# Seven products of blocks for the keys and values of two heads, in a decoder step with split-precision matmuls

## The chip, the core and the metric

The kernel runs on one core of one Trainium2 chip. The metric is the device time of one launch in microseconds, as the median of several runs. A core has a matmul engine (TensorE, PE in the profile), VectorE (DVE), ScalarE (ACT), GpSimd (POOL) and a queue that issues DMAs (SP). Each engine takes its instructions in the order in which they are written in its own queue, and waits at an instruction until what it needs has been signalled.

## The reference

One inference step of a decoder layer. A prompt of 512 tokens, with 16 meta tokens ahead of it, and 8 sequences of 4 new tokens go through one layer. All 560 tokens share one input projection:

```
h = RMSNorm_pre(x)
[q,k,v,ga | cb,cc,ch,gc | ma,mc] = h @ w_in          # 2048 x 12288
a = StickBreakingAttn(q,k,v) * silu(ga)              # 8 heads of 128
c = cb * conv3_causal(cc * ch) * silu(gc)
m = sigmoid(ma + b_ga) * (a @ w_pa) + sigmoid(mc + b_gc) * (c @ w_pc)
x = x + RMSNorm_post(m @ w_out)
```

The new tokens attend to cached keys and values in pages of 128, too. Keys and values of all tokens are outputs of their own, so k and v are computed for all 560 tokens; the other parts of the projection are needed for 544 (not for the meta tokens).

## The kernel before

**Precision.** Every float32 operand x of a matmul is split into a high part (ACT casts it, L240 for weights) and a low part (DVE subtracts, L241), and a product is three matmuls: high x high, high x low, low x high. h stands in two tiles, `h_hi` and `h_lo`, of 16 chunks of 128 rows by 560 tokens.

**Plain products.** `proj` (through `gemm_into`, L256) makes one tile of 128 columns of `w_in`: two blocks of weights of 1024 x 128 are loaded by SP into `raw`, split into `whi` and `wlo`, and 16 chunks x 3 matmuls are run for each half of the tokens, 280 columns wide. That is 96 matmuls. `k_proj` and `v_proj` evacuate the result into a tile `raw` of the pool `heads`, transpose it on PE (`natural`), write it out, and keep it in DRAM (`k_scr`, `vn_scr`) for attention later. Heads 0 to 3 attend at once (`head_now`); heads 4 to 7 are only projected here (`head_later`).

**Products of blocks.** From the gates on, two column tiles are made together by `pair` and `seven` (matmuls at L941): w_in's rows and columns and h's rows and tokens are cut in halves, and the 2 x 2 block product is done with seven block products in place of eight, each of 8 chunks x 3 = 24 matmuls. For this the weights are added up by DVE into `s` and in place (L953, L956, L964, L969), seven blocks are split in place of four, and three sums of blocks of h stand ready: `t_hi[i]`, `t_lo[i]`, i = 0 to 2. A fourth sum, `r1`, takes the place of one block of h itself (its rows 0 to 1023, second half of the tokens). In `seven`, two products go to PSUM tiles named mm and the others to the one tile named o, the accumulator y: first with t[0], then with t[1], then with t[2]. Results leave by ACT, or by a subtraction on DVE (L967, L972).

**The block sums** (L908 to L925) are made in four chunks c of two of the eight chunks of rows: nine additions or subtractions and three splits for t[0] to t[2], and at the end one split of r1 into h. That is 13 DVE instructions a chunk. The last split overwrites a block of h that `proj` reads, so it has to wait until the last plain product has read it.

**Decode.** The new tokens' logits against cached keys are made on DVE in 64 steps (L754), which `dec_step` puts between the pieces of the rest: the first part beside the heads (`"part"`), the second beside the gates. Later, beside the products with `w_pc`, PE multiplies the weights with the cached value pages (`vpage`, L841), 64 pages of 128 x 512, loaded by POOL from a pool with 7 buffers; the four sequences of a group write to four different parts of PSUM tile tp.

**Order.** The kernel is written as one program; a list scheduler of the framework orders each engine's queue by priorities and by its own estimate of times, so that work of a later piece can stand ahead of an earlier one. What the queues look like is known from the built program.

Of the kernel before, what the change touches and what calls it, by code (L numbers as in the profile page):

```python
# [9 lines left out]
F32 = mybir.dt.float32  # L10
# [38 lines left out]
SCRATCH = 4096  # L49
FIRST = 4  # L50
WARM = 10
NOW = 4
LNEXP = "natural_log_exp_and_others"
SCALE = P ** -0.5
# [6 lines left out]
def hybrid_step_kernel(  # L61
# [209 lines left out]
    def proj(c, ranges):  # L271
        return gemm(weights(win_srcs(c)), h_rhs, ranges)
# [285 lines left out]
        split_evac(vhi[0:16, 4, :], vlo[0:16, 4, :], vn[0:16, 4, :], vn[0:16, 4, :])  # L558
        return vhi, vlo

    def k_proj(h):
        o = proj(GATE_K + h * P, ALL)
        kr = hp.tile([P, T], F32, name="raw", bufs=2)
        for ob, s in nparts(o):
            act.copy(kr[:, s], ob)
        kn = hp.tile([P, 5, P], F32, name="nat", bufs=2)
        ks = hp.tile([TS, P], F32, name="ks", bufs=1)
        natural(kr, kn, ks)
        outputs(k_prompt, k_sample, h, kn, ks, pin if h == 0 else lambda x: x)
# [7 lines left out]
    def v_proj(h, pl=None):  # L577
        o = proj(GATE_V + h * P, ALL)
        vr = hp.tile([P, T], F32, name="raw", bufs=2)
        for ob, s in nparts(o):  # L580
            act.copy(vr[:, s], ob)
# [150 lines left out]
    def decode_steps():  # L732
# [89 lines left out]
        for g in range(2):  # L822
            for hf in range(2):
                cs = slice(hf * 512, (hf + 1) * 512)
                po = t_ps()
                for pg in range(NPG + 1):
                    if pg < NPG:
                        vts = []
                        for j in range(4):
                            vt = d3.tile([P, 512], F32, name="vpage", bufs=7)  # L830
                            page_load(vt, vc, 4 * g + j, pg, cs)
                            vts.append(vt)
                        if g + hf + pg == 0:
                            yield "values"
                    for j in range(4):
                        bb = 4 * g + j
                        if pg < NPG:
                            lhs, rhs = A_all[:, pg, bb].rearrange("p h t -> p (h t)"), vts[j]
                        else:
                            lhs, rhs = An[:, bb, :], vflat[:, cs]  # L840
                        pe.matmul(po[32 * j:32 * (j + 1), :], lhsT=lhs, rhs=rhs, start=(pg == 0),  # L841
                                  stop=(pg == NPG), tile_position=(0, 32 * j), skip_group_check=True)
# [13 lines left out]
                yield  # L856
# [25 lines left out]
    for h in range(NOW):  # L882
        head_now(h)
    nctx.close()
    for h in range(NOW, H):
        head_later(h)
    dec_step(64, "part")

# [3 lines left out]
    t_hi, t_lo = [], []  # L892
    for i in range(3):
        ttp = tctx.enter_context(tc.tile_pool(name=f"tt{i}", bufs=1))
        t_hi.append(ttp.tile([P, 8, HU], F32R, name=f"t_hi{i}"))
        t_lo.append(ttp.tile([P, 8, HU], F32R, name=f"t_lo{i}"))
    h_f, l_f = h_hi.bitcast(F32), h_lo.bitcast(F32)

    def blk(x, i, j):
        return x[:, 8 * i:8 * i + 8, (j + 1) * HC - HU:(j + 1) * HC]  # L900

    def t_split(hi, lo, x):
        act.copy(hi, x)
        dve.tensor_sub(lo, x, hi.bitcast(F32))

    with tc.tile_pool(name="tsum", bufs=2, side="right") as tsp:
        r1 = tsp.tile([P, 8, HU], F32, name="r1", bufs=1)
        for c in range(0, 8, 2):  # L908
            def part(x, *ij):
                return (blk(x, *ij) if ij else x)[:, c:c + 2]  # L910

            r, x, y = part(r1), *(tsp.tile([P, 2, HU], F32, name=n) for n in "xy")
            dve.tensor_sub(r, part(h_f, 0, 0), part(h_f, 0, 1))
            dve.tensor_add(r, r, part(l_f, 0, 0))
            dve.tensor_sub(r, r, part(l_f, 0, 1))
# [11 lines left out]
    hctx.close()  # L927


    def gate_out(j, w, g):  # L930
        pool.dma_start(gate_scr[j][:, w, :], g)

    def gate_bias(j, w):
        return bg[:, KD * w + j:KD * w + j + 1]

    def product(o, w, rhs, start, stop):
        hi, lo = w
# [44 lines left out]
    def pair(c, n):  # L982
# [4 lines left out]
            return lambda k: (h_hi[:, 8 * i + k, slice(*hs[j])], h_lo[:, 8 * i + k, slice(*hs[j])])  # L987

        def rt(i):
            return lambda k: (t_hi[i][:, k, HU - n:HU], t_lo[i][:, k, HU - n:HU])  # L990

        ws = blocks_of(win, c)
        s = sp2.tile([P, 8, P], F32, name="s")
        yield from seven(ws, n, rb, rt, s, lambda name: sp2.tile([P, HU], F32, name=name)[:, :n])

    gctx = ExitStack()
    gp = gctx.enter_context(tc.tile_pool(name="gates", bufs=2))
    sp2 = gctx.enter_context(tc.tile_pool(name="sums", bufs=1))


    UP, US = PQ + 2, DB * (DT + 2)
# [95 lines left out]
    dec_step(64, "values")  # L1097
    assert "values" in dec_at and "end" not in dec_at
    gctx.close()
    tctx.close()  # L1100


# [329 lines left out]
```

## Time and profile before

| | us |
|---|---|
| median of 3 runs | 1615.59 (1614.0 to 1616.18) |
| profiled execution | 1616.69 |
| its span, first to last instruction | 1615.1 |
| PE busy | 1595.0 |
| DVE busy | 1268.6 |
| ACT busy | 754.0 |
| first matmul of blocks (L941) | at 369.3 |

The profile is of one execution. A page gives busy times and groups of instructions with their line in the kernel before; the chain of waits is followed back from the last instruction. "out<-in" are the program's tiles. The profile's own time is 1.6 us longer than its span.

### The profile page before, as it was taken

The numbers are of one execution on the slowest core, as the hardware profiler recorded it, in microseconds if no ns is written. First come the engines' busy times: TensorE is split into PE (matmuls) and PEld (weight loads), VectorE is DVE, ScalarE is ACT, GpSimd is POOL, SyncE is SP. The second block draws the span as 40 slices with busy tenths as digits, with TensorE's granted clock in tenths as the row PEclk, the third lists the DMA queues.
The fourth block names the chain that finished last, engine by engine and source line by source line (L and its number), as shares of the span: only waits on it lengthen the run. The fifth ranks groups of instructions, "written<-read, shape, count | busy, mean of one in ns | idle before, by whom it ended". The sixth has DMA issues, their size and how long they took to land.

```text
span 1615.1 us, 32344 instructions
## 1 busy us (share of the span) xinstructions
PE 1595.0 (99%) x12172; PEld 1533.7 (95%) x12172; DVE 1268.6 (79%) x3574; ACT 754.0 (47%) x1339; POOL 238.0 (15%) x428
## 2 busy tenths in 40 slices
PE   9999999999999999999999999999999999999997
PEld 8999999999999999999999999999757789999997
DVE  6328999947899999999999986667565747887776
ACT  6335554435444444444454444446554523355562
POOL 1133333221111001001011100001322210000000
PEclk9999999999999999999999999999999999999999
DMA  8245555344554445454455544444966755533345
GB/s 244 85 139 179 162 173 177 114 121 142 163 166 138 137 139 164 119 151 133 139 171 183 155 145 128 130 127 124 334 218 222 232 152 162 173 88 110 99 133 187
DMA packets 300675, 252.77 MB, mean 157 GB/s; under 512 B 11522, under 2 KB 268614, under 8 KB 299702
## 3 DMA queue, kind: packets, MB, share of 16 engines
q1 hardware_dynamic: 272021, 160.45, 34.5%
q0 software_dynamic: 28368, 89.98, 16.8%
q8 instruction: 95, 1.56, 0.4%
q14 instruction: 63, 0.51, 0.1%
q10 hardware_dynamic: 128, 0.27, 0.1%
HBM read 217.95 MB, written 32.71 MB: 155 GB/s over the span
## 4 chain that ended last, share of the span: by engine, by line
PE 95%; DMA 2%; DVE 2%; ACT 1%; issue 0%; DVEq 0%; POOL 0%; SPq 0%; ACTq 0%
PE mm L941 31%; PE mm L256 27%; PE o L941 23%; PE tp L841 3%; PE mm L321 2%; PE z L677 1%; PE o L687 1%; PE z L321 1%; PE z L608 1%; PE z L1373 1%; DMA sg<-a_scr 1%; PE tp L505 0%; DMA raw<-in_w_pc 0%; DMA qb<-q_scr 0%; PE z L1227 0%
## 5 line engine op out<-in xcount | busy, mean ns | idle before, releaser
L240 ACT CAST whi<-raw 128x1024 fp32r<-128x1024 f32 x247 | 259.5, 1051 | 385.2 <-PE mm L941 118.5
L241 DVE TENSOR_TENSOR wlo<-raw,whi 128x1024 fp32r<-128x1024 f32 x247 | 301.8, 1223 | 87.8 <-ACT whi L240 86.5
L941 PE MATMUL mm<-h_hi,whi 128*128 128x272 f32 (+1 forms) x1152 | 332.3, 288 | 0.0
L941 PE MATMUL mm<-h_lo,whi 128*128 128x272 f32 (+1 forms) x1152 | 332.3, 288 | 0.0
L941 PE MATMUL mm<-h_hi,wlo 128*128 128x272 f32 (+1 forms) x1152 | 332.3, 290 | 0.0
L941 PE MATMUL o<-t_hi,whi 128*128 128x272 f32 (+1 forms) x864 | 250.1, 289 | 1.6 <-DVE c L967 1.6
L941 PE MATMUL o<-t_lo,whi 128*128 128x272 f32 (+1 forms) x864 | 250.2, 290 | 0.0
L754 DVE CUSTOM_DVE_ANT_0 junk<-kpage,qb 128x128 f32<-128x128 f32 x1024 | 246.3, 288 | 4.7 <-DMA qb<-q_scr 4.3
L941 PE MATMUL o<-t_hi,wlo 128*128 128x272 f32 (+1 forms) x864 | 249.8, 289 | 0.0
L941 PEld LDWEIGHTS mm<-h_hi,whi 128*128 128x128 f32 x1152 | 217.4, 189 | 0.0
L941 PEld LDWEIGHTS mm<-h_hi,wlo 128*128 128x128 f32 x1152 | 216.8, 189 | 0.1
L941 PEld LDWEIGHTS mm<-h_lo,whi 128*128 128x128 f32 x1152 | 216.8, 188 | 0.1
L241 DVE TENSOR_TENSOR wlo<-s,whi 128x1024 fp32r<-128x1024 f32 x126 | 154.4, 1225 | 63.6 <-ACT whi L240 62.4
L240 ACT CAST whi<-s 128x1024 fp32r<-128x1024 f32 x126 | 132.0, 1048 | 153.8 <-PE mm L941 51.7
L256 PE MATMUL mm<-h_lo,whi 128*128 128x280 f32 (+1 forms) x640 | 187.6, 293 | 0.0
L256 PE MATMUL mm<-h_hi,wlo 128*128 128x280 f32 (+1 forms) x640 | 187.1, 293 | 0.0
L256 PE MATMUL mm<-h_hi,whi 128*128 128x280 f32 (+1 forms) x640 | 186.7, 292 | 0.0
L941 PEld LDWEIGHTS o<-t_hi,whi 128*128 128x128 f32 x864 | 163.0, 189 | 2.1 <-DVE c L967 2.0
L941 PEld LDWEIGHTS o<-t_lo,whi 128*128 128x128 f32 x864 | 163.4, 189 | 0.4 <-issue 0.4
L941 PEld LDWEIGHTS o<-t_hi,wlo 128*128 128x128 f32 x864 | 163.1, 189 | 0.1
L256 PEld LDWEIGHTS mm<-h_lo,whi 128*128 128x128 f32 x640 | 120.3, 188 | 0.8
L256 PEld LDWEIGHTS mm<-h_hi,whi 128*128 128x128 f32 x640 | 120.5, 188 | 0.5
(390 smaller groups left out, 3214.5 us busy)
## 6 DMA issues: line engine op xcount, KB each, us to landing
raw<-in_w_in SPq DMA_DIRECT2D x192, 512.0 KB, 4.3
kpage<-in_cache_k POOLq DMA_DIRECT2D x64, 256.0 KB, 3.7
qb<-q_scr POOLq DMA_DIRECT2D x32, 512.0 KB, 5.7
vpage<-in_cache_v POOLq DMA_DIRECT2D x64, 256.0 KB, 5.4
raw<-in_w_out SPq DMA_DIRECT2D x32, 512.0 KB, 4.1
gate_scr<-g POOLq DMA_DIRECT2D x32, 272.0 KB, 4.8
gt<-gate_scr POOLq DMA_DIRECT2D x16, 544.0 KB, 4.5
raw<-in_w_pc SPq DMA_DIRECT2D x16, 512.0 KB, 7.3
```

The costliest lines, as they stand in the source:

```text
L240: act.copy(hi, x)
L241: dve.tensor_sub(lo, x, hi.bitcast(F32))
L256: pe.matmul(o, lhsT=w, rhs=r[:, t0:t1], start=(k == 0 and n == 0), stop=(k == nk - 1 and n == 2))
L321: pin(pe.matmul(o, lhsT=l, rhs=r[:, k, t0:t1], start=(start and m == 0), stop=(stop and m == 2), skip_group_check=True))
L608: pe.matmul(zt[:m, c0:c0 + n], lhsT=l[:, s0:s0 + m], rhs=r[:, ts:ts + n], start=(c0 == 0 and i == 0), stop=(i == 2), skip_group_check=True)
L677: pe.matmul(o, lhsT=l, rhs=x, start=False, stop=(i == len(ops) - 1), skip_group_check=True)
L687: pe.matmul(ot[:, ts - NMETA:ts - NMETA + n], lhsT=l[:m, st, :], rhs=x[:m, c0:c0 + n], start=False, stop=(g == GROUPS[-1] and i == 2), ski ...
L754: dve.tensor_tensor_reduce(out=junk, in0=kt[:, h * P:(h + 1) * P], in1=qt[:, t, h * P:(h + 1) * P], scale=1.0, scalar=0.0, op0=ALU.mult, o ...
L841: pe.matmul(po[32 * j:32 * (j + 1), :], lhsT=lhs, rhs=rhs, start=(pg == 0), stop=(pg == NPG), tile_position=(0, 32 * j), skip_group_check= ...
L941: pe.matmul(o, lhsT=l[:, k, :], rhs=r, start=(start and k == 0 and m == 0), stop=(stop and k == 7 and m == 2), skip_group_check=True)
L1373: pin(pe.matmul(o, lhsT=(m1, m2)[h][:, k + 8 * (q == 1), ts], rhs=two[h][q == 2][:, :, k, :], start=(n == 0), stop=(n == 47)))
```

## The change

- Heads 6 and 7 (`PAIRED = 6`) no longer go through `head_later`. A new function `two_heads` makes the keys of both with one call of `pair` over all 280 tokens of each half, and then the values of both; `k_proj` and `v_proj` take the finished tile.
- The block sums cover all 280 columns of a half, not 274, so that `pair` can be called with 280. They stand behind heads 4 and 5 in the program, ahead of heads 6 and 7; before, they stood behind all heads.
- The pool of `seven`'s small tiles (`sums`) is opened ahead of the paired heads, and its tiles and the t tiles are 280 wide. The pool `vpage` has 6 buffers in place of 7.

```diff
+PAIRED = 6
+    def whole(c):
+        r = hp.tile([P, T], F32, name="raw", bufs=2)
+        for ob, s in nparts(proj(c, ALL)):
+            act.copy(r[:, s], ob)
+        return r
-    def k_proj(h):
-        o = proj(GATE_K + h * P, ALL)
-        kr = hp.tile([P, T], F32, name="raw", bufs=2)
-        for ob, s in nparts(o):
-            act.copy(kr[:, s], ob)
+    def k_proj(h, kr=None):
+        kr = whole(GATE_K + h * P) if kr is None else kr
...
-                            vt = d3.tile([P, 512], F32, name="vpage", bufs=7)
+                            vt = d3.tile([P, 512], F32, name="vpage", bufs=6)
...
-    for h in range(NOW, H):
+    for h in range(NOW, PAIRED):
         head_later(h)
     dec_step(64, "part")
...
-        t_hi.append(ttp.tile([P, 8, HU], F32R, name=f"t_hi{i}"))
-        t_lo.append(ttp.tile([P, 8, HU], F32R, name=f"t_lo{i}"))
+        t_hi.append(ttp.tile([P, 8, HC], F32R, name=f"t_hi{i}"))
+        t_lo.append(ttp.tile([P, 8, HC], F32R, name=f"t_lo{i}"))
...
-        return x[:, 8 * i:8 * i + 8, (j + 1) * HC - HU:(j + 1) * HC]
+        return x[:, 8 * i:8 * i + 8, j * HC:(j + 1) * HC]
...
+    def two_heads(c):
+        rs = [hp.tile([P, T], F32, name="raw", bufs=2) for _ in range(2)]
+        for m, half, ob in pair(c, HC):
+            act.copy(rs[m][:, NMETA + half * HQ:NMETA + (half + 1) * HQ], ob[:, HM:HC])
+            act.copy(rs[m][:, half * HM:(half + 1) * HM], ob[:, 0:HM])
+        return rs
+    for h in range(PAIRED, H, 2):
+        for i, r in enumerate(two_heads(GATE_K + h * P)):
+            pool.dma_start(k_scr[h + i], k_proj(h + i, r))
+        for i, r in enumerate(two_heads(GATE_V + h * P)):
+            v_proj(h + i, vr=r)
+    hctx.close()
```

How the queues move, at three places. Line numbers in the rows of the change are its own, one to two above those of before up to the sums, and 5 below them in `seven`.

DVE, the end of the block sums, before. r_5282 is r1; t_lo_5268, _5273 and _5278 are the low halves of t[0], t[1] and t[2]; x and y are the sums under way; the splits of `wlo<-raw` are those of plain products of heads.

```order
L904 TENSOR_TENSOR t_lo_5278<-x,t_hi_5277 128x548 x2
L510 COPY nat<-tp 16x128
L511 COPY ks<-tp 32x128
L241 TENSOR_TENSOR wlo<-raw,whi 128x1024 x2
L510 COPY nat<-tp 16x128
L511 COPY ks<-tp 32x128
L241 TENSOR_TENSOR wlo<-raw,whi 128x1024 x2
L510 COPY nat<-tp 16x128
L511 COPY ks<-tp 32x128
L904 TENSOR_TENSOR h_lo<-r_5282,h_hi 128x2x274 x4
L953 TENSOR_TENSOR s<-raw 128x1024
L964 TENSOR_TENSOR raw<-raw 128x1024
```

DVE, where r1 is split into h, in the change (the middle of the sums). r_4744 is r1; t_lo_4730, _4735 and _4740 are the low halves of t[0], t[1] and t[2]; `s` and the splits `wlo<-s` belong to the paired heads.

```order
L906 TENSOR_TENSOR h_lo<-r_4744,h_hi 128x2x280
L924 TENSOR_TENSOR x<-h_hi,x 128x560
L242 TENSOR_TENSOR wlo<-s,whi 128x1024
L906 TENSOR_TENSOR h_lo<-r_4744,h_hi 128x2x280
L924 TENSOR_TENSOR x<-h_hi,x 128x560
L906 TENSOR_TENSOR t_lo_4735<-y,t_hi_4734 128x560 x2
L925 TENSOR_TENSOR x<-x,h_lo 128x560
L951 TENSOR_TENSOR s<-s,raw 128x1024
L925 TENSOR_TENSOR x<-x,h_lo 128x560
L511 COPY nat<-tp 16x128
L512 COPY ks<-tp 32x128
L906 TENSOR_TENSOR t_lo_4740<-x,t_hi_4739 128x560
```

Before, the splits of weights of two whole heads stand between the last split of t[2] and the four splits of r1 into h, and the additions of weights for the first pair come behind. Now the splits of r1, the additions and splits of weights for the paired heads and the rest of the sums are mixed.

PE, the third product of the paired heads' keys in the change (tile o, with t[0]); before, PE runs plain products of heads 5 and 6 at this place of its queue.

```order
L936 MATMUL mm<-h_hi,wlo 128x280
L936 MATMUL o<-t_hi_4729,whi 128x280
L936 MATMUL o<-t_lo_4730,whi 128x280
L936 MATMUL mm<-h_hi,whi 128x280
L936 MATMUL mm<-h_lo,whi 128x280
L936 MATMUL o<-t_hi_4729,wlo 128x280
```

The product with t[0] now stands in pieces between pieces of other products.

PE, the last pages and the new tokens of one group in the stage of `w_pc`, before:

```order
L256 MATMUL mm<-c_hl,wlo 128x272
L677 MATMUL z<-lo,neg_u 128x400
L841 MATMUL tp<-vpage,z_all 32x512 x4
L841 MATMUL tp<-v_new,z_new 32x512 x4
L256 MATMUL mm<-c_hl,whi 128x272 x2
```

and a place of that stage in the change:

```order
L257 MATMUL mm<-c_hl,whi 128x272 x2
L843 MATMUL tp<-vpage,z_all 32x512
L257 MATMUL mm<-c_hl,wlo 128x272
L257 MATMUL mm<-c_hl,whi 128x272 x2
L257 MATMUL mm<-c_hl,wlo 128x272
L257 MATMUL mm<-c_hl,whi 128x272
L843 MATMUL tp<-vpage,z_all 32x512
```

Groups of value pages that stood together now stand apart in several places, and some that stood apart stand together.

More of the change, by code (lines that the diff above doesn't have):

```diff
@@ L575, in k_proj, with v_proj @@
         return kr
[L577 to L581, printed above, removed]
+    def v_proj(h, pl=None, vr=None):
+        vr = whole(GATE_V + h * P) if vr is None else vr
         vn = hp.tile([P, 5, P], F32, name="nat", bufs=2)
@@ L906, in hybrid_step_kernel @@
     with tc.tile_pool(name="tsum", bufs=2, side="right") as tsp:
-        r1 = tsp.tile([P, 8, HU], F32, name="r1", bufs=1)
+        r1 = tsp.tile([P, 8, HC], F32, name="r1", bufs=1)
         for c in range(0, 8, 2):
@@ L910, in part @@
                 return (blk(x, *ij) if ij else x)[:, c:c + 2]
-            r, x, y = part(r1), *(tsp.tile([P, 2, HU], F32, name=n) for n in "xy")
+            r, x, y = part(r1), *(tsp.tile([P, 2, HC], F32, name=n) for n in "xy")
             dve.tensor_sub(r, part(h_f, 0, 0), part(h_f, 0, 1))
@@ L926, in hybrid_step_kernel @@
             t_split(blk(h_hi, 0, 1)[:, c:c + 2], blk(h_lo, 0, 1)[:, c:c + 2], r1[:, c:c + 2])
[L927 to L934, printed above, removed]
     def product(o, w, rhs, start, stop):
@@ L989, in rt, with gate_out, gate_bias @@
         def rt(i):
-            return lambda k: (t_hi[i][:, k, HU - n:HU], t_lo[i][:, k, HU - n:HU])
+            return lambda k: (t_hi[i][:, k, HC - n:HC], t_lo[i][:, k, HC - n:HC])
         ws = blocks_of(win, c)
         s = sp2.tile([P, 8, P], F32, name="s")
-        yield from seven(ws, n, rb, rt, s, lambda name: sp2.tile([P, HU], F32, name=name)[:, :n])
+        yield from seven(ws, n, rb, rt, s, lambda name: sp2.tile([P, HC], F32, name=name)[:, :n])
+    sctx = ExitStack()
+    sp2 = sctx.enter_context(tc.tile_pool(name="sums", bufs=1))
+    def two_heads(c):
[10 more added lines that the diff above has]
+    hctx.close()
+    def gate_out(j, w, g):
+        pool.dma_start(gate_scr[j][:, w, :], g)
+    def gate_bias(j, w):
+        return bg[:, KD * w + j:KD * w + j + 1]
     gctx = ExitStack()
     gp = gctx.enter_context(tc.tile_pool(name="gates", bufs=2))
-    sp2 = gctx.enter_context(tc.tile_pool(name="sums", bufs=1))
     UP, US = PQ + 2, DB * (DT + 2)
@@ L1099, in hybrid_step_kernel @@
     gctx.close()
+    sctx.close()
     tctx.close()
```

## The prediction

> **What bounds the kernel now.** I read the page first (its busy shares and its chain of waits), then the chain in order of time around the place of the change, then a table by stage, and last the groups of VectorE in that stage.
>
> ```profile
> span 1615.1 us, 32344 instructions
> PE 1595.0 (99%) x12172; PEld 1533.7 (95%) x12172; DVE 1268.6 (79%) x3574; ACT 754.0 (47%) x1339; POOL 238.0 (15%) x428
> PE 95%; DMA 2%; DVE 2%; ACT 1%; issue 0%; DVEq 0%; POOL 0%; SPq 0%; ACTq 0%
> ```
>
> TensorE (PE) is busy 99% of the span and carries 95% of the chain that ended last, so a matmul that goes away is worth its whole slot. VectorE (DVE) is second with 79%. An average over stages doesn't say whether it has room where it is given more; the rows of the stage do.
>
> ```profile
> 308.00 3.27 PE mm L256 x24
> 311.27 0.11 PE tp L508
> 311.38 0.11 PE tp L509
> 311.49 9.24 PE mm L256 x72
> 320.73 0.44 PE tp L505 x4
> 364.18 5.26 PE mm L256 x41
> 369.44 3.28 PE mm L941 x26
> 382.44 3.04 PE o L941 x24
> ```
>
> These are pieces of the chain (start, length, engine, what was written, line). PE runs without a hole from 308 to 369 us. 72 matmuls of 280 columns take 9.24 us, 0.128 us each. At 369.44 the plain products of the heads (L256) end and the products of blocks (L941) begin; 24 of those, of 272 columns, take 3.04 us, and 24 of 280 columns would take 24 x 0.128 = 3.08.
>
> ```profile
> 294.00:316.00 22.00, 22.00 (x172) 21.61 (x172) 20.85 (x37) 8.50 (x18) 6.51 (x11) 1.00 0.38 113
> 316.00:370.00 54.00, 54.00 (x424) 53.39 (x424) 29.93 (x44) 21.30 (x42) 11.96 (x20) 1.00 0.38 112
> ```
>
> The table by stage (length, then busy time and count of PE, PEld, DVE, ACT, POOL, then the granted clock): from 294 to 316 DVE has 1.1 us free, from 316 to 370 it has 24.1. It is this free time that the change fills.
>
> **The change part by part. PE.** Before, heads 6 and 7 take four projections of 96 matmuls, 384. After, two pairs of seven products of 24 matmuls, 336. 48 x 0.128 = **6.2 us less on the path**. The transposes and the small logits product of each head stay. The weights loaded are the same eight blocks of 512 KB, on SP's queue as before; POOL's queue gets the same output writes of these heads, and the decode's next loads still stand behind them.
>
> **DVE, how much.** Its groups from 294 to 370 us (count, busy, mean ns, idle before them), then four rows of its timeline:
>
> ```profile
> L241 DVE TENSOR_TENSOR wlo<-raw,whi 128x1024 fp32r<-128x1024 f32 x10 | 12.2, 1217 | 9.1 <-ACT whi L240 9.1
> L904 DVE TENSOR_TENSOR t_lo<-x,t_hi 128x548 fp32r<-128x548 f32 x8 | 5.7, 719 | 1.4 <-ACT t_hi L903 1.4
> L904 DVE TENSOR_TENSOR h_lo<-r,h_hi 128x548 fp32r<-128x548 f32 x4 | 2.9, 724 | 0.3 <-ACT h_hi L903 0.2
> L913 DVE TENSOR_TENSOR r<-h_hi 128x548 f32<-128x548 f32 x4 | 2.7, 724 | 0.0
> L953 DVE TENSOR_TENSOR s<-raw 128x1024 f32<-128x1024 f32 x1 | 1.2, 1226 | 0.0
> 294.34 2.65 DVE L913 TENSOR_TENSOR r<-h_hi 128x548 f32<-128x548 f32 x4
> 298.19 0.27 DVE L510 COPY nat<-tp 16x128 f32<-16x128 f32 x1
> 298.39 0.27 DVE L511 COPY ks<-tp 32x128 f32<-32x128 f32 x1
> 301.78 1.20 DVE L241 TENSOR_TENSOR wlo<-raw,whi 128x1024 fp32r<-128x1024 f32 x1
> 302.91 0.71 DVE L915 TENSOR_TENSOR r<-r,h_lo 128x548 f32<-128x548 f32 x1
> ```
>
> Durations overlap by their tails, so I take starts: four steps of a sum in 2.65 us with 0.72 for the last are (2.65 - 0.72) / 3 = 0.64 us each; a full weight block, split (L241) or added (L953, of the same length), is 302.91 - 301.78 = 1.13; a small copy 0.20. A sum step over 560 elements in place of 548 is 0.64 x 560 / 548 = 0.66. There are 52 of them (13 lines over four chunks): 34.2 us after, 33.4 before. For heads 6 and 7 DVE had 8 splits, 9.0 us; it gets 14 splits and 8 additions, 24.9, and four subtractions of half a sum step's width, some 1.3 (my estimate, from 0.64). That is 17.2 + 0.8 = 18 us more in a stage that is to be 6.2 us shorter and had 24 to 25 us free. In total it fits almost exactly; what decides is when each piece is due.
>
> **DVE, by when.** PE takes heads 4 and 5 in the order of before, whose last matmul stands 41 behind the transposes that end at 311.49: 311.49 + 41 x 0.128 = 316.7 us. From there to the end of the second product that reads a block sum (t[1]) the new order has 146 matmuls and six transposes: 146 x 0.128 + 0.44 + 0.22 = 19.4, so an unhindered PE wants the last of t[1] just before 336.1. DVE is an in-order queue. The sums began at 294.34; now two additions of weight blocks and two copies stand ahead of them (2 x 1.13 + 0.4), so they begin at 297.0. From there to the last low half of t[1] the order has 51 sum steps, 8 splits, 4 additions and 4 copies: 51 x 0.66 + 12 x 1.13 + 4 x 0.20 = 48.0, so 345.0 with no wait at all. Five matmuls follow, 0.64 us: 345.6 against 336.1, **a stall of 9.5 us at least**. The splits of the paired heads stand among the sums because PE needs both; before, the last four sum steps (the rows h_lo) were done when PE got there, and no head waited for a sum.
>
> DVE will also wait now and then. Before, the sums waited 1.4 + 0.3 us for ScalarE and ten splits 9.1 (those mostly because DVE was early). Bounds: none, or 9.1 / 10 for each of 8 splits plus 1.7, which is 9. A queue that is behind waits little, so I take 3, nearer the first: **stall 12.5 us, bounds 6 to 18** (6 where PE is given later work to do in the holes). Behind PE's wait stand the second pair's products and everything after; nothing makes it up, as PE has no other holes.
>
> **Granted clock.** One stall of the old trace shows what follows one (timeline of PE, then the table by stage):
>
> ```profile
> 1149.36 1.91 PE L841 MATMUL tp<-vpage,z_all 128*32 128x512 f32 x12
> 1154.53 0.82 PE L256 MATMUL mm<-c_hl,whi 128*128 128x272 f32 x2 [3.25 <-DVE gt L1148]
> 1158.10 1.04 PE L841 MATMUL tp<-vpage,z_all 128*32 128x512 f32 x2
> 1159.08 0.81 PE L608 MATMUL z<-qhi,khi 128*128 128x400 f32 x3
> 1155.00:1158.00 3.00, 3.00 (x16) 2.94 (x15) 3.00 (x6) 0.00 (x0) 2.16 (x4) 0.56 0.99 327
> ```
>
> After 3.25 us without a matmul the granted clock is 0.56 for three microseconds, a loss of 3 x (1 - 0.56) = 1.3 us. The new stall is cut into holes between bursts, since the products of t[0] come in pieces; and while PE waits for DVE anyway, a slow clock costs nothing. Bounds 0 and two such losses, 2.6; I take 0.5. [...]
>
> **The decode's value pages.** vpage has six buffers for seven, and the page products on PE come in other groups. The rows above price a group: the single page (two records) at 1158.10 holds PE until 1159.08, 0.98 us; six pages (twelve records) take 1.91. Up to four pages in a row run side by side and cost one slot. The old order has 34 runs of up to four pages and 6 longer, 34 x 0.98 + 6 x 1.91 = 44.8 us; the new one 40 and 4, 46.8: **2.0 us more**. What later loads add:
>
> ```profile
> POOL vpage L730 <- PE tp L841: 74.6, 27, 10.4
> L841 PE MATMUL tp<-vpage,z_all x128: 592/592/617, 1149.4 to 1296.5; 128*32 128x512 f32 x128
> DMA to landing us min/median/max: 2.8/5.4/7.6
> ```
>
> The loads already wait 27 times for a buffer, 74.6 us in all; the view of these products names no DMA among what PE waited for. With a buffer less each load is issued one page later; over 1149.4 to 1296.5 there are 64 pages, one in 2.3 us, against 5.4 to land. Bounds: a gain of 1, if groups fall better than counted, and a wait of 3.3, as long as the one hole of that stage. I add nothing.
>
> **Sum.** -6.2 + 12.5 + 0.5 + 2.0 = +8.8 us. The profiled execution took 1616.7 us (span 1615.1 and 1.6 around it); the median of the runs shown is 1615.6, 1.1 below it. So 1625.5 for a profiled execution and **1624.4** as a median.
>
> **The rivals.**
>
> *DVE keeps up.* If the sums are early enough, only the 48 matmuls count: 1615.6 - 6.2 = 1609.4. For it: 24.1 us free on DVE from 316 to 370, and the total fits. Against it: the queue is in order and 48 us of rows stand ahead of a product due 39 us after they begin. It would take sum steps of 0.47 us, and every row here shows 0.64. Chance 0.10.
>
> *A draw.* The second pair's products fill holes, the stall is 4 to 9 us and the pages cost nothing: 1613 to 1618, say 1615.6. For it: the order already puts one of the second pair's products ahead of the stalled one. Chance 0.13, with the faint chance that the change does not reach PE as counted included; the order shows 39 rows less on PE, and that its 48 matmuls are gone.
>
> *Clock and pages on top.* The stall leaves a hole of over 3 us more than once, each followed by a slow stretch (+2.1 over my 0.5), and late pages put a second hole of 3.3 into the value stage: 1624.4 + 2.1 + 3.3 = 1629.8, and more with a stall near 18. [...] Chance 0.17.
>
> *The forecast,* a stall of 9.5 to 15 us: 0.60, its own range 1619 to 1629.
>
> **How the numbers follow.** About 0.2% (3.2 us) is what a measurement of this kernel tells from no change. Slower by more: the forecast, the third rival and a little of the draw, 0.81; same 0.10, most of the draw; faster 0.09, nearly all of the first rival. The range leaves out most of the first rival and the far end of the third: 1613 to 1631.
>
> **What would show it.** In the table by stage of the changed kernel DVE is busy nearly without a hole from about 297 to 340 us, while PE has holes of 10 us or more between 317 and 348, released by DVE (low halves of t[0] and t[1], splits of s). The first gate product (272 columns) starts near 376 in place of 369.4. The page products hold some 47 us. I am wrong if PE shows no holes there (then DVE's rows came faster or in another order), or if the holes are there and the end is not later, which would mean that a later stage had slack I did not see.

## The result, and the profile after

| | before | after |
|---|---|---|
| median of six runs each, us | 1615.36 (1614.0 to 1616.59) | 1624.46 (1622.06 to 1630.77) |
| ratio after to before | | 1.0065, 95% interval 1.0046 to 1.0084 |
| span of the profiled execution, us | 1615.1 | 1629.2 |

The change costs 9.1 us. The profiled execution of the changed kernel took 1630.77 us, the longest of its six runs and 6.3 above their median. Its later part therefore shows more than the change costs: the last section says what that is. The stretch of the change comes first, and is read from where it begins.

The page of the changed kernel, span and chain:

```profile
span 1629.2 us, 32289 instructions
PE 1599.0 (98%) x12124; PEld 1533.2 (94%) x12124; DVE 1288.4 (79%) x3592; ACT 761.8 (47%) x1351; POOL 234.5 (14%) x428
PE 95%; DVE 2%; DMA 2%; ACT 1%; issue 1%; DVEq 0%; SPq 0%; ACTq 0%
```

48 matmul records fewer, and yet PE is busy 4 us longer: part of its time ran at a lower clock (0.987 on the mean over the span, before 0.997). The table by stage of the changed kernel (length, then busy time and count of PE, PEld, DVE, ACT, POOL, then granted clock, DMA share, GB/s):

```profile
294.00:316.00 22.00, 22.00 (x174) 21.70 (x173) 21.02 (x35) 10.52 (x22) 4.93 (x9) 1.00 0.26 82
316.00:335.00 19.00, 12.95 (x87) 11.26 (x86) 18.63 (x26) 8.60 (x14) 3.59 (x6) 0.95 0.42 114
335.00:350.00 15.00, 13.16 (x71) 12.93 (x72) 12.34 (x16) 5.64 (x10) 0.00 (x0) 0.72 0.12 35
350.00:378.00 28.00, 28.00 (x224) 27.69 (x223) 18.94 (x22) 14.07 (x29) 5.83 (x10) 1.00 0.48 137
```

Before, PE had no hole in 316 to 370 and DVE had 24 us free there. Now DVE works without a hole from 295.5 to 345.8, but for 0.4 us, while PE stands 6.05 us in the second row and 1.84 in the third, and the clock is down. PE's timeline, the rows that begin after a hole of 0.4 us or more (in brackets the hole and what ended it; for the first the profile names nothing but issue), and the first and the last of the stretch of the paired heads: the first product of 280 columns, and the first of 272, where the gates begin.

```profile
314.12 0.28 PE L936 MATMUL mm<-h_hi,whi 128*128 128x280 f32 x1
...
323.13 0.37 PE L936 MATMUL o<-t_hi,whi 128*128 128x280 f32 x1 [2.03 <-issue]
...
324.03 0.40 PE L936 MATMUL mm<-h_hi,whi 128*128 128x280 f32 x1 [0.41 <-ACT whi L241]
...
329.75 0.39 PE L936 MATMUL o<-t_hi,whi 128*128 128x280 f32 x1 [0.53 <-ACT t_hi L905]
...
331.67 0.40 PE L936 MATMUL o<-t_lo,whi 128*128 128x280 f32 x1 [1.53 <-DVE t_lo L906]
...
333.66 0.60 PE L936 MATMUL o<-t_hi,whi 128*128 128x280 f32 x1 [0.82 <-ACT t_hi L905]
...
334.76 0.60 PE L936 MATMUL mm<-h_hi,wlo 128*128 128x280 f32 x1 [0.50 <-DVE wlo L242]
...
342.71 0.40 PE L936 MATMUL mm<-h_hi,whi 128*128 128x280 f32 x1 [1.84 <-ACT whi L241]
...
373.92 0.29 PE L936 MATMUL mm<-h_hi,whi 128*128 128x272 f32 x1
```

With one more of 0.24 the holes come to 7.9 us. The stretch from 314.12 to 373.92 takes 59.8 us, and this is the number by which the experiments are compared. DVE's timeline in the same kernel, the begin of the sums, a split of weights, the last low half of t[1] right behind it, and the first result after them:

```profile
295.53 2.68 DVE L915 TENSOR_TENSOR r<-h_hi 128x560 f32<-128x560 f32 x4
...
342.11 1.22 DVE L242 TENSOR_TENSOR wlo<-raw,whi 128x1024 fp32r<-128x1024 f32 x1
343.24 0.73 DVE L906 TENSOR_TENSOR t_lo<-y,t_hi 128x560 fp32r<-128x560 f32 x1
...
347.92 0.45 DVE L962 TENSOR_TENSOR c<-o,s 128x280 f32<-128x280 f32 x1 [2.16 <-PE o L936]
```

From the first sum to the last low half of t[1] DVE works 48.4 us, and only after that, at 347.92, does it wait for PE. Of PE's holes 2.3 us end with DVE itself and 1.4 with ACT's copies (t_hi) of sums that DVE delivers. The first two, 2.4 us together, are of another kind. ACT, too, takes its queue in order, and ahead of the next weights stands its copy of a finished product, which waits for PE (ACT's timeline):

```profile
321.14 0.39 ACT L954 COPY s<-mm 128x280 f32<-128x280 f32 x1 [2.73 <-PE mm L936]
```

Behind it come one more high half and then the weights, done at 323.04; PE goes on at 323.13. The runs below with early sums keep 1.2 and 1.7 us of this. The hole of 1.84 ends with ACT's weights as well, but it costs nothing of its own: right behind it PE needs the split that DVE ends at 342.11 + 1.22 = 343.33, and takes it up at once (PE's timeline):

```profile
343.37 0.33 PE L936 MATMUL o<-t_hi,wlo 128*128 128x280 f32 x1
```

This is the third of the 24 matmuls of the product with t[1]; the twentieth is the first to need the last low half, which is ready at 343.97. The granted clock, in the stretches that the trace gives at half rate:

```profile
333.20:340.10 6.90, 5.94 (x24) 5.63 (x25) 6.90 (x10) 1.07 (x2) 0.00 (x0) 0.51 0.00 0
343.40:346.90 3.50, 3.50 (x17) 3.50 (x17) 2.37 (x3) 0.11 (x1) 0.00 (x0) 0.51 0.51 150
715.50:722.40 6.90, 6.24 (x27) 6.25 (x28) 5.95 (x20) 0.58 (x1) 0.00 (x0) 0.51 0.26 76
1162.60:1169.50 6.90, 6.20 (x26) 6.10 (x27) 5.11 (x10) 0.62 (x1) 2.15 (x4) 0.51 0.92 289
```

The first two lie in the stretch of the change: PE does 9.4 us of work there that takes 4.7 at full rate. The other two lie far behind it.

### The profile page after: what moved, and what is told of

It reads as the page before. It is cut to its first block, busy times and chain, and to the rows that moved or that the text cites. A ratio compares the mean times of both kernels' runs of the same rounds, so it can differ in the third digit from the quotient of the medians.

```text
span 1629.2 us, 32289 instructions
## 1 busy us (share of the span) xinstructions
PE 1599.0 (98%) x12124; PEld 1533.2 (94%) x12124; DVE 1288.4 (79%) x3592; ACT 761.8 (47%) x1351; POOL 234.5 (14%) x428
## 4 chain that ended last, share of the span: by engine, by line
PE 95%; DVE 2%; DMA 2%; ACT 1%; issue 1%; DVEq 0%; SPq 0%; ACTq 0%
PE mm L936 33%; PE o L936 24%; PE mm L257 24%; PE tp L843 3%; PE mm L322 2%; PE z L679 1%; PE o L689 1%; PE z L322 1%; PE z L610 1%; PE z L1392 1%; DMA sg<-a_scr 1%; DMA raw<-in_w_in 0%; PE tp L506 0%; DMA raw<-in_w_pc 0%; PE z L1246 0%
## 5 line engine op out<-in xcount | busy, mean ns | idle before, releaser
L936 PE MATMUL mm<-h_hi,whi 128*128 128x272 f32 (+2 forms) x1216 | 352.9, 290 | 2.2 <-ACT whi L241 2.2
L936 PE MATMUL mm<-h_hi,wlo 128*128 128x272 f32 (+2 forms) x1216 | 352.7, 291 | 0.7 <-DVE wlo L242 0.7
L936 PE MATMUL mm<-h_lo,whi 128*128 128x272 f32 (+2 forms) x1216 | 352.4, 290 | 0.0
L936 PE MATMUL o<-t_hi,whi 128*128 128x272 f32 (+2 forms) x912 | 266.2, 292 | 6.6 <-DVE c L962 3.2
L936 PE MATMUL o<-t_lo,whi 128*128 128x272 f32 (+2 forms) x912 | 265.3, 291 | 1.5 <-DVE t_lo L906 1.5
L936 PE MATMUL o<-t_hi,wlo 128*128 128x272 f32 (+2 forms) x912 | 265.9, 292 | 0.0
L936 PEld LDWEIGHTS mm<-h_hi,whi 128*128 128x128 f32 x1216 | 230.9, 190 | 2.9 <-ACT whi L241 2.9
L936 PEld LDWEIGHTS mm<-h_lo,whi 128*128 128x128 f32 x1216 | 230.0, 189 | 0.1
L257 PE MATMUL mm<-c_hl,whi 128*128 128x272 f32 x512 | 107.0, 298 | 3.3 <-DVE gt L1167 3.3
L257 PEld LDWEIGHTS mm<-c_hl,whi 128*128 128x128 f32 x512 | 84.1, 193 | 25.7 <-issue 21.0
```

The lines of the kernel that those rows point to most:

```text
L257: pe.matmul(o, lhsT=w, rhs=r[:, t0:t1], start=(k == 0 and n == 0), stop=(k == nk - 1 and n == 2))
L936: pe.matmul(o, lhsT=l[:, k, :], rhs=r, start=(start and k == 0 and m == 0), stop=(stop and k == 7 and m == 2), skip_group_check=True)
```

## The experiments

Each was timed beside runs of the kernel before on its own chip. Differences are of the medians; intervals are of the ratio.

| run | us | runs | against before, us | ratio, 95% interval |
|---|---|---|---|---|
| the change | 1624.46 | 6 | +9.1 | 1.0046 to 1.0084 |
| before, six page buffers | 1618.52 | 8 | +4.2 | 1.0017 to 1.0038 |
| change, seven page buffers | 1620.13 | 5 | +5.8 | 1.0030 to 1.0057 |
| change, decode work put off | 1610.93 | 11 | -3.4 | 0.9964 to 0.9985 |
| change, only the values paired | 1612.59 | 11 | -1.7 | 0.9984 to 1.0002 |
| change, sums without low parts | 1611.53 | 10 | -3.2 | 0.9971 to 0.9990 |
| decode put off, DVE work repeated | 1630.23 | 4 | +15.8 | 1.0079 to 1.0110 |
| change, low halves on GpSimd | 1629.89 | 4 | +15.2 | 1.0073 to 1.0106 |
| decode put off, seven buffers | 1607.39 | 6 | -7.1 | 0.9946 to 0.9973 |
| decode put off, eight buffers | 1603.77 | 6 | -10.7 | 0.9908 to 0.9942 |
| before, eight buffers | 1611.56 | 10 | -2.9 | 0.9968 to 0.9987 |

**Is the vector queue what is late?** The theory: DVE is in order, and 48 us of rows stand ahead of a product that PE wants sooner. Two runs take work from it in different ways, and leave PE's matmuls alone. The first puts off decode work: of the 64 logits steps, 16 instead of 24 come beside the heads, and 48 instead of 40 are spread over the gates.

```diff
-DEC1 = 6
+DEC1 = 4
...
-            dec_step((0, 2, 2, 2)[n - 1] if n <= 4 else 1 if n <= 20 else 1 + n % 2, "logits")
+            dec_step((0, 2, 2, 2)[n - 1] if n <= 4 else 1 if n <= 20
+                     else 26 * (n - 20) // 12 - 26 * (n - 21) // 12, "logits")
```

> The changed kernel with 16 decode steps beside the heads in place of 24 (DEC1 = 4; the 8 others go to the later gates, where DVE has room). This takes 8 x 16 small reductions, some 27 us of DVE, away ahead of the block sums, and leaves PE's work as it is. Theory (DVE's in-order queue is late with the sums): the sums are done in time, PE's holes from 317 to 350 go, and the stage ends 6 us earlier than before in place of 5 later: 1615.4 - 6.2 + 2 (pages) = 1611, bounds 1608 to 1615. Rival (the holes come from the products of blocks themselves: one PSUM tile o for y, results that leave by ScalarE, weights that arrive late): the holes stay, 1624.

It took 1610.93 us, and the stretch of the paired heads has one hole. A row of its table by stage:

```profile
316.00:335.00 19.00, 17.82 (x139) 17.55 (x139) 15.89 (x19) 9.17 (x17) 3.60 (x6) 1.00 0.41 114
```

DVE's timeline, first sum and last low half of t[1]:

```profile
242.14 2.69 DVE L915 TENSOR_TENSOR r<-h_hi 128x560 f32<-128x560 f32 x4
...
316.89 0.72 DVE L906 TENSOR_TENSOR t_lo<-y,t_hi 128x560 fp32r<-128x560 f32 x1
```

PE's timeline, the first product of the stretch, the one after the hole, and the first of 272 columns:

```profile
316.73 0.28 PE L936 MATMUL mm<-h_hi,whi 128*128 128x280 f32 x1
...
325.15 0.39 PE L936 MATMUL mm<-h_hi,whi 128*128 128x280 f32 x1 [1.18 <-ACT whi L241]
...
364.05 0.29 PE L936 MATMUL mm<-h_hi,whi 128*128 128x272 f32 x1
```

The sums begin at 242 instead of 295, t[1] is whole at 317.6 instead of 344.0, and the stretch takes 364.05 - 316.73 = 47.3 us instead of 59.8. The 12.5 us between them are the 12.5 by which the run is faster (from 9.1 above before to 3.4 below). So close an agreement is in part chance: in the run with seven page buffers below, whose stretch has the same order as the change, it took 58.2. The hole of 1.18 is what is left of the rival: the products of blocks have a hole of their own, but a small one.

Putting off decode work also changes what ACT and POOL do beside the heads. So the second run leaves all of that where the change has it, and takes 20 of the DVE instructions out of the sums themselves:

```diff
             dve.tensor_sub(r, part(h_f, 0, 0), part(h_f, 0, 1))
-            dve.tensor_add(r, r, part(l_f, 0, 0))
-            dve.tensor_sub(r, r, part(l_f, 0, 1))
             dve.tensor_add(x, r, part(h_f, 1, 1))
-            dve.tensor_add(x, x, part(l_f, 1, 1))
...
-            dve.tensor_add(y, y, part(l_f, 0, 0))
...
-            dve.tensor_add(x, x, part(l_f, 1, 0))
```

> The changed kernel with the five additions of the low parts left out of each piece of the block sums: 20 DVE instructions of 0.65 us fewer, 13 us, while the decode work stays where the change has it. The sums, and so the outputs, lack the low parts of h. Theory (the vector queue is late by its own work): the last low half of the second sum comes 12 to 13 us earlier, near 331, before PE wants it; the time falls by 10 to 13 us to 1611 to 1615 us, as when decode work was put off. Rival (the decode work costs PE or ACT time where it stands, whatever the vector engine does): 1622 to 1626 us.

Measured 1611.53 us, 12.3 us under the change by the differences from before, and the stretch is 49.6 us, by PE's timeline and then DVE's for the last low half of t[1]:

```profile
312.97 0.28 PE L931 MATMUL mm<-h_hi,whi 128*128 128x280 f32 x1
...
321.21 0.37 PE L931 MATMUL o<-t_hi,whi 128*128 128x280 f32 x1 [1.25 <-issue]
...
322.11 0.60 PE L931 MATMUL mm<-h_hi,whi 128*128 128x280 f32 x1 [0.41 <-ACT whi L241]
...
362.57 0.29 PE L931 MATMUL mm<-h_hi,whi 128*128 128x272 f32 x1
```

```profile
318.40 0.72 DVE L906 TENSOR_TENSOR t_lo<-y,t_hi 128x560 fp32r<-128x560 f32 x1
```

The two holes left are those behind ACT's copy, 1.7 us, and the clock then runs at half rate from 322.2 to 325.6; this accounts for the 2.3 us over 47.3. But t[1] is whole at 319.1, not near 331 as expected: 24.9 us earlier, by an edit that removes 13 us. The sums begin where they did (294.4), but the scheduler also put eight of the twelve splits and additions of weights that stood ahead of t[1] behind it. So the run doesn't measure what 13 us on DVE are worth. It shows that with the decode work left in its place, and the sums early, PE's stall is gone: what the decode work cost was its place ahead of the sums, not time on PE or ACT, and that rival falls.

A third run adds DVE work to the run with decode put off, as a test from the other side:

```diff
+            for _ in range(10):
                 dve.tensor_sub(r, part(h_f, 0, 0), part(h_f, 0, 1))
```

> The kernel with decode work put off (1610.9 us), with the first subtraction of each of the four pieces of the block sums done ten times instead of once: 36 more DVE instructions of 0.65 us, 23.5 us, and nothing else changed. Theory (the vector queue is in order and sets when the second block sum is there): its last low half, ready at 317.6 us in the run without them, comes at 341; PE, whose block products begin at 316.7, wants it 14.7 to 19.4 us after that, at 331.4 to 336.1; PE then stands 5 to 10 us for it, some 3 us more for conversions behind it, and the time is 1618 to 1624 us. Rival (the gain of putting decode work off lay on PE or ACT, and the vector queue has slack): 1610 to 1612 us.

It took 1630.23 us, 19 over the run without the repeats and 6 over the range expected. The direction is the theory's, the size is not, and DVE's timeline says why:

```profile
322.70 1.22 DVE L242 TENSOR_TENSOR wlo<-raw,whi 128x1024 fp32r<-128x1024 f32 x1 [3.50 <-ACT whi L241]
...
328.42 1.23 DVE L242 TENSOR_TENSOR wlo<-s,whi 128x1024 fp32r<-128x1024 f32 x1 [4.11 <-ACT whi L241]
...
348.74 0.73 DVE L906 TENSOR_TENSOR t_lo<-y,t_hi 128x560 fp32r<-128x560 f32 x1
```

The scheduler wrote another order. The rest of the sums now stands behind splits of weights that wait for ACT, so DVE stands idle for 3.5 and 4.1 us and then has the sums to do; t[1] is whole at 349.5, not 341. PE's holes in the stretch come to 12.5 us, one of them of 6.0, and the clock is at half rate for 20.5 us of it. The run shows that late sums cost PE dearly; it doesn't measure what one microsecond on DVE costs, since the order was not held.

**Can another engine take the work?** The 16 subtractions of low halves go to GpSimd:

```diff
     def t_split(hi, lo, x):
         act.copy(hi, x)
-        dve.tensor_sub(lo, x, hi.bitcast(F32))
+        pool.tensor_sub(lo, x, hi.bitcast(F32))
```

> The changed kernel with the 16 subtractions that make the low halves of the block sums (the line after the copy to the high half) on GpSimd instead of DVE. DVE loses 16 x 0.65 = 10.4 us before the block products. No such instruction on GpSimd is in the profile; the nearest row is a 128x128 select of 0.38 to 0.49 us, which for 560 columns would be 1.7 to 2.1 us, 27 to 34 us for 16, beside 14 us of issues in that stretch. If GpSimd keeps up (the last low half of the second sum before 336): 1612 to 1615 us. If it does not, PE waits for GpSimd instead: 27 to 34 us from 300 on and the issues between them end at 340 to 350, and the time is 1619 to 1630 us.

Measured 1629.89 us, 6 us slower than the change (by the differences from before), and the stretch 66.1 us. The time lies in the range for a GpSimd that doesn't keep up, but neither of the two cases expected named the cause. POOL's timeline:

```profile
313.86 1.40 POOL L906 TENSOR_TENSOR t_lo<-x,t_hi 128x560 fp32r<-128x560 f32 x1
315.22 4.02 POOL L906 TENSOR_TENSOR h_lo<-r,h_hi 128x560 fp32r<-128x560 f32 x3
319.21 2.67 POOL L906 TENSOR_TENSOR t_lo<-y,t_hi 128x560 fp32r<-128x560 f32 x2
```

DVE's, and PE's, at the same place:

```profile
313.56 9.40 DVE L242 TENSOR_TENSOR wlo<-s,whi 128x1024 fp32r<-128x1024 f32 x1
```

```profile
323.02 0.60 PE L936 MATMUL mm<-h_hi,wlo 128*128 128x280 f32 x1 [6.63 <-DVE wlo L242]
```

GpSimd's instruction is cheaper than thought, 1.34 us each in a row. But while GpSimd runs six in a row, from 313.86 to 321.88, one split on DVE takes 9.40 us, where one of the same size at 303.28 took 1.21, and PE stands 6.63 us for it. The other long hole, of 4.66 us at 347.48, ends with ACT, which had itself waited 2.85 us for a sum of DVE's. In that stretch the work was not moved beside DVE but in front of it.

**The page buffers.** The kernel before with the changed buffer count alone:

```diff
-                            vt = d3.tile([P, 512], F32, name="vpage", bufs=7)
+                            vt = d3.tile([P, 512], F32, name="vpage", bufs=6)
```

> The kernel before with one edit: the pool of value pages has 6 buffers in place of 7; nothing else moves ahead of that stage. Theory (the pages cost by how they are grouped on PE): the queue now has 40 page groups of one slot and 4 of two, as the changed kernel has, 46.8 us in place of 44.8, so about 2 us over before (1617.4), 0 to 5. Rival (the later stage is longer in the changed kernel only because it comes at another time): no change, 1615.4.

1618.52 us: 4.2 above the kernel before, interval 2.7 to 6.1. And the changed kernel with its seventh buffer given back, for which tile `u` of the convolution gets a pool of its own that is closed ahead of the pages:

```diff
+    with tc.tile_pool(name="conv", bufs=2) as up_pool:
-    for i in range(0, 8, 2):
-        conv_pair(i)
+        for i in range(0, 8, 2):
+            conv_pair(i)
...
-        us_ = [gp.tile([P, UP + US], F32, name="u", bufs=2) for _ in range(2)]
+        us_ = [up_pool.tile([P, UP + US], F32, name="u", bufs=2) for _ in range(2)]
```

> The changed kernel with 7 page buffers again; room for them comes from putting the tile u of the convolution in a pool of its own that is closed after it. Theory: 2 us less than the changed kernel, 1622.5, bounds 1619 to 1624; the holes of PE from 317 to 350 us stay. Rival (buffers don't matter): 1624.5.

1620.13 us, 3.3 less than the change by the differences from before; PE's holes in the stretch stay (2.03, 1.52, 0.82, 0.50, 1.65 and a smaller one), as expected. The two runs agree within their intervals: the buffer is worth 3 to 4 us, some 40% of the whole loss. The page products show part of it. The groups on PE, of the kernel before with six buffers:

```profile
L841 PE MATMUL tp<-vpage,z_all 128*32 128x512 f32 x128 | 44.9, 604 | 0.0
```

And of the change with seven:

```profile
L843 PE MATMUL tp<-vpage,z_all 128*32 128x512 f32 x128 | 42.4, 603 | 0.0
```

(The change itself has 44.9 too, before had 42.4.) The same 128 records of the same mean length cover 2.5 us less with seven: they overlap in fewer groups (runs of their records with no other matmul between: 38 in the trace of before, with seven buffers, and 42 in that of the change, with six). The stage from the last product of the gates to the first with `w_out` took 282.4 us before and 286.0 with six buffers, and of these 3.6 us 1.7 are in the slots of page products, 0.9 in transposes and small products beside them, and 1.0 in products with `w_pc`, which come out longer by no cause that these traces show.

**Only the values paired.** Keys of heads 6 and 7 stay plain and the values are made by seven products, with six page buffers:

```diff
+    for h in range(PAIRED, H):
+        pool.dma_start(k_scr[h], k_proj(h))
...
-        for i, r in enumerate(two_heads(GATE_K + h * P)):
-            pool.dma_start(k_scr[h + i], k_proj(h + i, r))
```

> The changed kernel with the keys of heads 6 and 7 plain again, beside the sums, and only their values by seven products: half of the saving, 24 matmuls or 3.1 us, and DVE has two projections (24.6 us of PE) more to make the sums in. Theory (lateness of DVE): no holes, 1615.4 - 3.1 + 2 (pages) = 1614, bounds 1611 to 1617. Rival (a pair of heads costs more than it saves, by its evacuations and the chain through y): half of the loss, 1620.

1612.59 us, inside the range expected. The plain keys give DVE the time it lacks: a row of the table by stage, and DVE's timeline for the last low half of t[1].

```profile
316.00:335.00 19.00, 19.00 (x151) 18.70 (x150) 16.99 (x27) 8.07 (x18) 5.15 (x9) 1.00 0.39 116
```

```profile
332.13 0.73 DVE L908 TENSOR_TENSOR t_lo<-y,t_hi 128x560 fp32r<-128x560 f32 x1
```

t[1] is whole at 332.9, PE begins the paired products only at 339.3, and it has no hole. Half of the saving without the stall makes a kernel that is level with the one before, in spite of its missing buffer. It stands 5.9 us below the kernel before with six buffers, where its 24 matmuls account for 3.1; where the rest comes from is not shown.

**The parts put together.** Decode work put off and seven page buffers (both edits above), then the same with eight, and eight buffers for the kernel before:

> The kernel with decode work put off (DEC1 = 4, which ran in 1610.9 us) with seven page buffers instead of six; the convolution's tile u moves into a pool of its own, closed before the value pages come. If the page term is a matter of buffers alone and adds to the rest, it gives back what it cost the kernel before (4.2 us): 1606.7 us, between 1605 and 1609. If the page term were the 2.0 us of the forecast's group slots: 1609. If the two do not add (the pages are hidden once the decode groups come later): 1611.

> As the run with seven, with eight page buffers, two whole groups of four. Theory of groups: a group of four products lies in one slot of 0.98 us when its four pages are there, and 32 such slots take 31 us where seven buffers take 44.8 us in 34 and 6 slots, less what waits remain: 6 to 9 us under the run with seven buffers, 1598 to 1601 us. Rival, the transfers of the pages set the pace: no more than 1 us under the run with seven buffers, 1606 us.

> The kernel before with eight page buffers and nothing else (tile u in a pool of its own): the control for the run of eight. Theory of groups: 6 to 9 us under the kernel before, 1605 to 1609 us. Rival, transfers set the pace: 1613 to 1615 us.

Seven buffers give 1607.39 us, inside the range expected for terms that add: the saving, the stall and the buffer add up as separate terms. Eight give 3.6 us more, at 1603.77, and 2.9 for the kernel before, less than the 6 to 9 of the theory of groups and more than the 1 of its rival. Of the run with eight buffers and decode put off, PE's group of page products:

```profile
L843 PE MATMUL tp<-vpage,z_all 128*32 128x512 f32 x128 | 35.8, 609 | 0.0
```

PE's timeline, the row after its hole:

```profile
1264.58 0.79 PE L679 MATMUL z<-loA,neg_u 128*128 128x512 f32 x1 [3.63 <-DVE loA L496]
```

DVE's timeline ahead of it, and the table by stage for what follows:

```profile
1263.07 0.44 DVE L1168 TENSOR_TENSOR gt<-mm,gt 128x272 f32<-128x272 f32 x1 [4.70 <-DMA gt<-gate_scr]
...
1263.86 0.67 DVE L496 TENSOR_TENSOR loA<-rA,hiA 128x512 fp32r<-128x512 f32 x1
```

```profile
1263.90:1274.10 10.20, 9.52 (x39) 8.98 (x39) 4.89 (x13) 3.28 (x6) 2.69 (x5) 0.50 0.67 210
```

The groups are as the theory has them: 42.4 us become 35.8. But with the pages out of the way PE comes sooner to a product of an attention head, whose low half stands on DVE behind a gate factor that waits for its load. PE stands 3.63 us, then runs at half rate for 10.2 us, a loss of 4.8. The same hole, 3.38 us, is in the profiled execution of the kernel before with eight buffers. In this execution the load took back more (8.4 us) than the groups gave (6.6). But it was the slowest of its six (1612.66 us, 8.9 above their median), so the others lost less; how much, and so what held the median to 3.6, is not shown.

## Why the prediction was right, step by step

**PE, -6.2.** Right. The kernel before and the run with decode put off ran level at 110 us (DVE's timeline, of before, then of that run):

```profile
110.08 0.28 DVE L510 COPY nat<-tp 16x128 f32<-16x128 f32 x1 [2.50 <-PE tp L509]
```

```profile
110.09 0.28 DVE L511 COPY nat<-tp 16x128 f32<-16x128 f32 x1 [2.50 <-PE tp L510]
```

The gates begin at 369.44 before by the chain, where 26 products are one piece, and the first of 272 columns in it at 369.27; there it is 364.05, with a hole of 1.18: 5.2 + 1.2 = 6.4 us. In times, the run stands 7.6 us below the kernel before with six page buffers, and the intervals of the two runs leave room for 6.2.

**DVE, how much and by when, 12.5.** Right in its mechanism; the size held in part by luck. The sums began at 295.5 (predicted 297.0) and t[1] was whole at 344.0 (345.0), 48.4 us of rows where 48.0 were added up. The heads ended at 314.1 and not 316.7, since the program's first 110 us went 2.5 us quicker in this execution; so PE would have ended the product with t[1] at 333.5, where the forecast had 336.1. The last low half of t[1] alone, with its five matmuls, puts that end at 344.6: 11.1 late, where the rows of the forecast gave 9.5. What came last was another piece of DVE's queue, which the forecast counted but gave no due time: the split of the weights for this product, one row ahead of that low half. Only 5 matmuls wait for the low half, but 22 for the split, so with its end at 343.33 the product could not end before 346.2, 12.7 late (by the length of the stretch, 13.7 too long with 1.7 of it the clock's, 12.0). The 3 us that were added for waits of DVE's own did not occur (its rows waited 0.4 us in all); the 1.6 us of a later start and the 1.5 of this split took their place. The forecast expected holes of 10 us or more. They are 7.9, because PE spent part of the wait on later products at half rate.

**Granted clock, 0.5.** The term that was mis-sized. The stretch was at half rate for 10.2 us, a loss of 4.7. Some 3 of these hide in the wait for DVE's split; 1.7 lie behind it, from 343.5 to 346.9. That a stall cut into holes between bursts would cost little of the clock was the author's estimate, and no trace showed it; the clock fell at 333.2, after a hole of 1.53 and within one of 0.82, and again at 343.5, after one of 1.84. The loss after the one hole of the kernel before was read too small as well: there the trace has half rate from 1154.2 to 1157.6, 1.7 us lost, of which the row from 1155 to 1158 shows 1.3. Holes and clock together are 12.6 us, and the stretch is 12.5 longer than with decode put off (13.7 longer than if that run had no hole): the sum of the two terms, 13.0, holds, the clock's share of it does not.

**Value pages, 2.0.** Too small: 4.2 by the run with six buffers, 3.3 by the run with seven. Both lie within its bounds, which allowed from 1 less to 3.3 more than the 2.0. The count of groups was right (page products 44.9 us in place of 42.4 in the table of groups, 2.5 more). What failed is "I add nothing": the stage is longer by another 1 to 2 us beside the page products.

**Sum, +8.8.** -6.4 + 13.7 + 3.7 (the mean of the two page runs) = +11.0 by the traces; measured +9.1, interval 7.4 to 13.6. That the forecast came within 0.3 us of the measured median is luck in part: its page term was 1.7 too small, and the six runs of the change spread over 8.7 us.

**The rivals.** "DVE keeps up" predicted 1609.4; with the sums early, the run measured 1610.9 with six buffers and 1607.4 with seven, so its price was right and its condition false. The argument against it held: time that is free on an average does not help an instruction that stands behind 48 us of others. "Clock and pages on top" has the time of the profiled execution (1630.77 for 1629.8) but not its way: no hole of the stall passed 3 us, and what came on top were two half-rate stretches of 6.9 us far behind it, at 715 and at 1162, the second after a hole ended by a gate factor on DVE, not by a page. "A draw" expected a stall of 4 to 9 us and pages that cost nothing; neither was so.

**The marks.** DVE busy without a hole from 297 to 340: yes. PE's holes between 317 and 348, by DVE: in part. They are 7.9 us in place of 10; 3.6 end with DVE or ACT's copies of its sums, 2.4 are those behind ACT's copy of a product, and 1.8 end with weights on ACT just ahead of DVE's split. First gate product near 376: 373.9, 2.1 early, of which 2.5 are the quicker start. Page products some 47 us: 44.9 by the groups, 45.4 by starts.

## What to carry to other kernels

Work for an engine with free time must be costed at its place in that engine's queue: begin, rows ahead of the due piece, end, against the moment at which the other engine wants it. Here that sum put t[1] right to 1 us, where the average (24 us free for 18) said the opposite. Every piece ahead of the due one has a due time of its own: the split of weights, needed 22 matmuls before the product's end, was later than the sum itself. Where a change fails by lateness, look at what stands ahead in the same queue before giving it up: here eight decode steps moved to a later stage turned +9.1 into -3.4, and one page buffer given back with them made it -7.1.

## What the runs showed of the hardware

**The granted clock changed in steps of 3.413 us, not at the holes.** In the traces of the kernel before and of the change, each change of the granted clock lies a whole multiple of 3.413 us behind the one before it. In the change it falls at 333.23, rises at 340.06, falls at 343.47, rises at 346.88, and falls again at 715.52 and 1162.67. Before, it falls at 1154.20, which is not a whole number of steps from these: the phase differs. The same hole of the same stage, ahead of a product with `w_pc`, in the change and in the change with seven buffers (timeline of PE, then the table by stage for the second):

```profile
1163.30 0.82 PE L257 MATMUL mm<-c_hl,whi 128*128 128x272 f32 x2 [3.32 <-DVE gt L1167]
```

```profile
1156.61 0.52 PE L257 MATMUL mm<-c_hl,whi 128*128 128x272 f32 x2 [3.23 <-DVE gt L1168]
```

```profile
1158.00:1161.00 3.00, 3.00 (x18) 1.97 (x17) 3.00 (x6) 0.00 (x0) 2.00 (x4) 1.00 0.91 297
```

In the first, 2.7 us of the hole lay in the step that ends at 1162.67, and the clock was halved for the two steps behind it (1162.67 to 1169.50, a row above). In the second the hole is nearly as long, and the clock stayed at 1.00 behind it; why is not shown. Counted from the changes of the clock in the two traces, from 20 us after the start to the last matmul, the clock fell after the one step of before in which PE stood 2.93 us, and in the change after steps in which it stood 1.84, 1.92, 2.07 and 2.69 us, in some of them several holes together; it did not fall after one with 1.89. No other step at full rate has as much as 0.9. So these traces give no one length from which it falls. The start is another matter: in the change the clock fell at 8.97 us, after a step in which the trace shows no hole. What such a fall costs follows from the rows: the change's profiled execution did 6.24 + 6.20 us of work at half rate at 715 and 1162, a loss of 6.2 us, and the execution with seven buffers, whose mean clock was 0.993, lost nothing behind its hole of 3.23 us. That is as much as the profiled execution lay above its median (6.3); that this is the whole reason is inferred, since the other executions left no trace.

**A split on DVE took 9.40 us while GpSimd ran.** By the rows of the run with the low halves on GpSimd it began at 313.56, 0.30 us ahead of the first of six GpSimd instructions without a pause, and ended at 322.96, 1.08 us behind the end of the last; at 303.28 a split of the same size had taken 1.21 us. Beside a single GpSimd instruction another split took 2.41 us (DVE's timeline, then POOL's):

```profile
328.43 2.41 DVE L242 TENSOR_TENSOR wlo<-raw,whi 128x1024 fp32r<-128x1024 f32 x1
```

```profile
328.15 1.61 POOL L906 TENSOR_TENSOR t_lo<-x,t_hi 128x560 fp32r<-128x560 f32 x1 [2.15 <-ACT t_hi L905]
```

What held the two splits, the first of which began ahead of GpSimd, is not shown.
